# Max-unpooling on one core: the images dealt out in two contiguous parts of 384 and 640, five loads and three stores in place of three and four

## The chip, the core and the metric

The kernel runs on one core of a Trainium2 chip. The metric is device time in microseconds (us) of one execution; nine runs of the kernel before are at hand, and one more execution that was profiled.

## What is computed

The reference undoes a 2x2 max-pooling. Each input value goes to one of four places of a 2x2 block of the output, chosen by its index; the other three places are zero.

```python
output = np.zeros((batch, channels, 2 * h, 2 * w), dtype=np.float32)
for b, c, i, j in ...:
    idx = indices[b, c, i, j]
    output[b, c, 2 * i + idx // 2, 2 * j + idx % 2] = x[b, c, i, j]
```

There are 16 x 64 = 1024 images of 32 x 32 = 1024 values. Per image `x` is 4 KB of float32, the indices are 8 KB, since they lie in HBM as 64-bit integers, and the output is 16 KB. Together 12.58 MB are read and 16.78 MB written.

## The kernel before

**Layout.** Each of the 128 partitions holds `T = 8` consecutive images (L-numbers here are those of the profile). So `x` is one stretch of 32 KB per partition, the indices one of 64 KB, the output one of 128 KB. The whole input fits into the on-chip memory: `x_t` and `idx_t` hold it, and three tiles `out_t` hold two images of output each; the fourth group of two uses the first tile again.

**Loads.** Three DMAs, all on SyncE's queue (SP), are put ahead of SP's preamble by `program.first`: the indices of the first three images of every partition (L110, 24 KB per partition, semaphore `idx_in[0]`), all of `x` (L114, 32 KB per partition, `x_in`), and the indices of the other five images (L116, 40 KB per partition, `idx_in[1]`). In HBM, the rows of L110 and L116 begin 64 KB apart.

**Work.** VectorE waits for `x_in` (L121) and for `idx_in[0]` (L126). Then it walks over the images. For each of the four places of the 2x2 block one `scalar_tensor_tensor` (L137) compares the index with the place's number and multiplies the outcome with `x`, so that the value or a zero lands in a strided part of the output tile. One instruction takes two images (128x2048 elements), but at image 2 and at image 3 it takes one (128x1024), since the second load of indices begins with image 3 and its wait (again L126) stands there. That makes 12 instructions of two images and 8 of one. Ahead of the fourth group VectorE waits until the first store has landed (L132, `stored_0`), since the group writes into the first store's tile. The last instruction of each group raises `made`.

**Stores.** SP waits for `made` to reach 1, 2, 3 and 4, and after each wait issues one store (L150) of two images per partition: 32 KB per partition, rows 128 KB apart in HBM, 4.19 MB in all. At last it lowers `made` (L153), and the wait for the last three stores (L155) is moved to the program's end by `program.last`.

So one queue, SP's, carries all seven transfers in the order of their issue: three loads, four stores. Two things order the work: the loads' landing, for which VectorE waits, and `made`, for which SP waits.

Of the kernel before, what the change touches and what calls it, by code (L numbers as in the profile page):

```python
# [1 line left out]

# [4 lines left out]

P = 128
F32 = mybir.dt.float32
I32 = mybir.dt.int32  # L10


class Program:

    def __init__(self, nc):
        self.nc = nc
        self.block = nc.main_func.blocks[0]  # L20
        self.kernel_block = nc.cur_bb.bb.name

    def __enter__(self):
        ins = self.block.instructions
        self.branches = [i for i in ins if "Branch" in type(i).__name__]
        n = len(ins) - len(self.branches)
        assert all("Branch" in type(ins[k]).__name__ for k in range(n, len(ins)))
        del ins[n:]
        self.nc.switch_bb(self.block.name, parent=None)
        self.symbolic = self.nc._always_lower_symbolic_ap  # L30
        self.nc._always_lower_symbolic_ap = False
        return self

    def first(self, made):
        ins = self.block.instructions
        assert ins[len(ins) - 1].name == made.ins.name
        moved = ins.pop()
        at = next(
            k
            for k, i in enumerate(ins)  # L40
            if i.engine == moved.engine and isinstance(i, mybir.InstDrain)
        )
        ins.insert(at, moved)

    def last(self, made):


        def move(nc):
            ins = self.block.instructions
            at = next(k for k, i in enumerate(ins) if i.name == made.ins.name)  # L50
            nc.main_func.blocks[-1].instructions.append(ins.pop(at))

        self.nc.at_finalize(move)

    def __exit__(self, kind, *_):
        self.nc._always_lower_symbolic_ap = self.symbolic
        if kind is None:
            for b in self.branches:
                self.block.instructions.append(b)
            self.nc.switch_bb(self.kernel_block, parent=None)  # L60


@with_exitstack
def kernel(
    ctx: ExitStack,
    tc: tile.TileContext,
    x: bass.AP,
    indices: bass.AP,
    kernel_size: bass.AP,
    out: bass.AP,  # L70
):
    nc = tc.nc
    assert kernel_size == 2

    B, C, H, W = x.shape
    n_img = B * C
    T = n_img // P
    assert T * P == n_img and C % T == 0

    G = 2  # L80
    NG = T // G
    FIRST = 3
    N = H * W
    x_v = x.rearrange("b (ch t) h w -> (b ch) (t h w)", t=T)
    idx_v = indices.rearrange("b (ch t) h w -> (b ch) (t h w)", t=T).bitcast(I32)
    out_v = out.rearrange("b (ch g t) oh ow -> g (b ch) (t oh ow)", g=NG, t=G)

    x_t = nc.alloc_sbuf_tensor("x_t", [P, T * N], F32).ap()
    idx_t = nc.alloc_sbuf_tensor("idx_t", [P, T * 2 * N], I32).ap()
    out_t = [  # L90
        nc.alloc_sbuf_tensor(f"out_t{g}", [P, G * 4 * N], F32).ap()
        for g in range(NG - 1)
    ]
    out_t.append(out_t[0])

    x_in = nc.alloc_semaphore("x_in")
    idx_in = [nc.alloc_semaphore(f"idx_in{g}") for g in range(2)]
    made = nc.alloc_semaphore("made")
    stored_0 = nc.alloc_semaphore("stored_0")
    stored = nc.alloc_semaphore("stored")  # L100

    x_c = x_t.rearrange("p (t i j) -> p t i j", t=T, j=W)
    idx_c = idx_t.rearrange("p (t i j two) -> p t i j two", t=T, j=W, two=2)[
        :, :, :, :, 0
    ]
    cut = FIRST * 2 * N

    with Program(nc) as program:
        program.first(
            nc.sync.dma_start(out=idx_t[:, :cut], in_=idx_v[:, :cut]).then_inc(  # L110
                idx_in[0], 16
            )
        )
        program.first(nc.sync.dma_start(out=x_t, in_=x_v).then_inc(x_in, 16))  # L114
        program.first(
            nc.sync.dma_start(out=idx_t[:, cut:], in_=idx_v[:, cut:]).then_inc(  # L116
                idx_in[1], 16
            )
        )

        nc.vector.wait_ge(x_in, 16).then_inc(x_in, -16)  # L121
        for t in range(T):
            g, k = t // G, t % G
            if t in (0, FIRST):
                half = int(t == FIRST)
                nc.vector.wait_ge(idx_in[half], 16).then_inc(idx_in[half], -16)  # L126

            if k == 1 and t != FIRST:
                continue
            n = 1 if k == 1 or t + 1 == FIRST else 2  # L130
            if g == NG - 1:
                nc.vector.wait_ge(stored_0, 16).then_inc(stored_0, -16)  # L132
            o_c = out_t[g].rearrange(
                "p (m i two j wo) -> p m i two j wo", m=G, two=2, wo=2, j=W
            )
            for pidx in range(4):
                op = nc.vector.scalar_tensor_tensor(  # L137
                    out=o_c[:, k : k + n, :, pidx // 2, :, pidx % 2],
                    in0=idx_c[:, t : t + n],
                    scalar=pidx,  # L140
                    in1=x_c[:, t : t + n],
                    op0=mybir.AluOpType.is_equal,
                    op1=mybir.AluOpType.mult,
                )
            if k + n == G:
                op.then_inc(made, 1)

        for g in range(NG):
            nc.sync.wait_ge(made, g + 1)
            nc.sync.dma_start(out=out_v[g], in_=out_t[g]).then_inc(  # L150
                stored if g else stored_0, 16
            )
        nc.sync.sem_inc(made, -NG)  # L153
        program.last(
            nc.sync.wait_ge(stored, 16 * (NG - 1)).then_inc(stored, -16 * (NG - 1))  # L155
        )


# [1 line left out]
_INS = ['x', 'indices', 'kernel_size']  # L160
_OUTS = [((16, 64, 64, 64), 'float32')]

_NUMBERS = {'kernel_size': 2}


# [26 lines left out]
```

## Time and profile before

| what | value |
|---|---|
| median of 9 runs | 71.49 us (71.41 to 71.64) |
| the profiled execution: its own time | 71.5 us |
| its span, first to last instruction | 70.2 us |
| VectorE busy, 20 instructions | 35.6 us |
| loads issued at | 0.00, 0.43, 0.90 us |
| from issue to landing of the loads | 9.5, 18.8, 30.5 us |
| stores issued at | 28.4, 37.5, 46.3, 55.1 us |
| from issue to landing of the stores | 12.8, 13.3, 14.2, 15.1 us |

All times in the profile count from the start of the span, which is the issue of the first load. 1.3 us of the execution's own time lie outside of the span. A DMA's landing is the moment at which its completion has raised its semaphore: its issue plus the time to landing.

### The profile page before, as it was taken

To read this page: it belongs to the slowest core of one execution; us is meant where nothing else is said; L and a number is where in the kernel's file an instruction comes from. 1 tells how busy PE (TensorE), PEld (TensorE's weight loads), DVE (VectorE), ACT (ScalarE), POOL (GpSimd) and SP (SyncE) were. 2 spreads that over 40 slices of the span, in tenths; PEclk is the share of its full clock that TensorE was granted. 3 is DMA by queue.
4 is the path that set the end of the run, shared out by engine and by line. 5 is a ranking of instruction groups with operands and counts; after the bars stand their busy time and mean duration, and the time that the engine had idled before them with its cause. 6 is when DMAs were issued, how large, how long until landed. Compare 5 with 4: busy or idle time off the path is not lost.

```text
span 70.2 us, 72 instructions
## 1 busy us (share of the span) xinstructions
DVE 35.6 (51%) x20; POOL 0.2 (0%) x4
## 2 busy tenths in 40 slices
DVE  0000000000099999999999999999999300000000
POOL 1000000000000000000000000000000000000000
DMA  8699996969988999869799797969799897969790
GB/s 224 294 420 434 439 579 299 598 299 523 448 374 374 420 607 467 374 299 560 336 411 486 336 560 318 579 299 579 318 486 411 355 542 336 560 299 579 318 560 37
DMA packets 1008, 29.36 MB, mean 418 GB/s; under 512 B 112, under 2 KB 112, under 8 KB 112
## 3 DMA queue, kind: packets, MB, share of 16 engines
q1 hardware_dynamic: 1008, 29.36, 97.7%
HBM read 12.58 MB, written 16.78 MB: 418 GB/s over the span
## 4 chain that ended last, share of the span: by engine, by line
DVE 46%; DVEq 4%; issue 1%
DVE out_t L137 46%; DVEq L187 4%
## 5 line engine op out<-in xcount | busy, mean ns | idle before, releaser
L137 DVE SCALAR_TENSOR_TENSOR out_t<-idx_t,x_t 128x2048 f32<-128x2048 int32 (+1 forms) x20 | 35.6, 1856 | 19.5 <-DVEq L126 19.5
L173 POOL MEMSET const-uint8-127<- 128x1 uint8 x1 | 0.1, 103 | 0.0
L173 POOL MEMSET const-bfloat16-1.0<- 128x1 bf16 x1 | 0.1, 102 | 0.0
L173 POOL MEMSET const-float32-0.0<- 128x1 f32 x1 | 0.1, 99 | 0.2 <-issue 0.2
L173 POOL MEMSET const-float32-1.0<- 128x1 f32 x1 | 0.1, 99 | 0.0
## 6 DMA issues: line engine op xcount, KB each, us to landing
out_dram<-out_t SPq DMA_DIRECT2D x4, 4096.0 KB, 13.8
idx_t<-in_indices_dram SPq DMA_DIRECT2D x1, 5120.0 KB, 30.5
x_t<-in_x_dram SPq DMA_DIRECT2D x1, 4096.0 KB, 18.8
idx_t<-in_indices_dram SPq DMA_DIRECT2D x1, 3072.0 KB, 9.5
```

What stands on the lines that cost most here:

```text
L137: op = nc.vector.scalar_tensor_tensor(out=o_c[:, k : k + n, :, pidx // 2, :, pidx % 2], in0=idx_c[:, t : t + n], scalar=pidx, in1=x_c[:, t ...
L173: nc = _bacc.Bacc("TRN2", target_bir_lowering=False, num_devices=1)
L187: with _tile.TileContext(nc) as tc:
```

## The change

The images are dealt out to partitions in two parts. Part A is images 0 to 383, three consecutive images per partition; part Z is images 384 to 1023, five per partition. Each part is one unbroken piece of HBM for `x`, for the indices and for the output.

The loads become five, all ahead of SP's preamble as before: indices of A (24 KB per partition) and `x` of A (12 KB), both on semaphore `in_a`; `x` of Z (20 KB) and the indices of the first four images of Z (32 KB), both on `in_z`; the indices of the last image of Z (8 KB, `in_last`).

VectorE's work becomes four steps of four instructions: three images of A after `in_a`; two images of Z after `in_z`; two more, after a wait for its own `made` to reach 2; the last image after `in_last`. That is 4 instructions of 128x3072, 8 of 128x2048 and 4 of 128x1024.

The stores become three: all of A (48 KB per partition, 6.29 MB), the first two images of Z (32 KB, 4.19 MB), and the last three of Z (48 KB, 6.29 MB). Ahead of the first, SP waits for `in_z` besides `made`. The output of the last three lies over input that is used up by then (the whole of A's and the indices of the first two images of Z), in place of an output tile that waits for a store to land; so VectorE's wait for the first store is gone.

```diff
-        nc.vector.wait_ge(x_in, 16).then_inc(x_in, -16)
-        for t in range(T):
-            g, k = t // G, t % G
-            if t in (0, FIRST):
-                half = int(t == FIRST)
-                nc.vector.wait_ge(idx_in[half], 16).then_inc(idx_in[half], -16)
...
-            n = 1 if k == 1 or t + 1 == FIRST else 2
-            if g == NG - 1:
-                nc.vector.wait_ge(stored_0, 16).then_inc(stored_0, -16)
...
+    work = (
+        (x_a, idx_a, 0, A, 0, 0),
+        (x_z, idx_z, 0, Z1, 1, 0),
+        (x_z, idx_z, Z1, Z2 - 1, 2, 0),
+        (x_z, idx_z, Z - 1, 1, 2, Z2 - 1),
+    )
...
+        for tile_, hbm, sem in (
+            (idx_a, idx_v[0], in_a),
+            (x_a, x_v[0], in_a),
+            (x_z, x_v[1], in_z),
+            (idx_z[:, :last_idx], idx_v[1][:, :last_idx], in_z),
+            (idx_z[:, last_idx:], idx_v[1][:, last_idx:], in_last),
+        ):
+            program.first(nc.sync.dma_start(out=tile_, in_=hbm).then_inc(sem, 16))
+
+        for k, (x_s, idx_s, lo, n, o, at) in enumerate(work):
+            if k == 0:
+                nc.vector.wait_ge(in_a, 32).then_inc(in_a, -32)
+            elif k == 1:
+                nc.vector.wait_ge(in_z, 32)
+            elif k == 2:
+                nc.vector.wait_ge(made, 2)
+            else:
+                nc.vector.wait_ge(in_last, 16).then_inc(in_last, -16)
...
-            if k + n == G:
+            if k != 2:
                 op.then_inc(made, 1)
...
+        for k, dst in enumerate(stores):
+            nc.sync.wait_ge(made, k + 1)
+            if k == 0:
+                nc.sync.wait_ge(in_z, 32)
+            nc.sync.dma_start(out=dst, in_=out_t[k]).then_inc(stored, 16)
+        nc.sync.sem_inc(made, -3)
+        nc.sync.sem_inc(in_z, -32)
+        program.last(nc.sync.wait_ge(stored, 48).then_inc(stored, -48))
```

## The prediction

> **What bounds the kernel now.** I first read the head of the page, the transfers' queue and the slices.
>
> ```profile
> span 70.2 us, 72 instructions
> DVE 35.6 (51%) x20; POOL 0.2 (0%) x4
> DMA  8699996969988999869799797969799897969790
> q1 hardware_dynamic: 1008, 29.36, 97.7%
> ```
>
> VectorE (DVE) works half of the span; the one DMA queue keeps the 16 DMA engines busy for 97.7% of it. The slices' sixes are no holes, since a packet here is a whole row of 24 to 40 KB, counted whole in a slice; longer stretches show it:
>
> ```profile
> 0.00:2.00 2.00, 0.00 (x0) 0.20 (x4) 1.00 0.73 197
> 10.00:20.00 10.00, 0.54 (x1) 0.00 (x0) 1.00 1.00 433
> 20.00:30.00 10.00, 10.00 (x6) 0.00 (x0) 1.00 1.05 455
> 30.00:40.00 10.00, 10.00 (x9) 0.00 (x0) 1.00 0.97 419
> 40.00:50.00 10.00, 10.00 (x5) 0.00 (x0) 1.00 0.99 426
> 50.00:60.00 10.00, 5.05 (x3) 0.00 (x0) 1.00 1.07 462
> 68.00:70.20 2.20, 0.00 (x0) 0.00 (x0) 1.00 0.56 238
> ```
>
> The last two columns are DMA share and GB/s. The share stays near 1.00 and the rate near 440 from loads (10 to 30) through to stores (30 to 60); only start and end are slack. Then the chain and the waits:
>
> ```profile
> by line: DVE out_t L137 46.3%; DVEq L187 3.8%; issue 0.8%
> ```
>
> ```profile
> SPq L150 <- DVE out_t L137: 52.3, 4, 26.7
> SPq L155 <- SPq L155: 14.0, 1, 14.0
> ```
>
> The chain names VectorE, but it only follows instructions. The last store is issued at 55.1 us and lands 15.1 us later, though it has 4.19 MB like the first load of x: it stands behind the third store in the queue. So VectorE is not what ends last. The landings are the real clock: 9.5 for the first indices (3.15 MB), 0.43 + 18.8 = 19.2 for x, 0.9 + 30.5 = 31.4 for the other indices, then 28.4 + 12.8 = 41.2, 37.5 + 13.3 = 50.8, 46.3 + 14.2 = 60.5, 55.1 + 15.1 = 70.2. Between them lie 9.7, 12.2, 9.8, 9.6, 9.7, 9.7 us for 4.19, 5.24 and four times 4.19 MB. From 9.5 to 70.2, 26.21 MB move in 60.7 us: **432 GB/s** without a break. That is the price of a byte below.
>
> [...] The rows here are 64 and 128 KB apart[...], and the trace shows no loss from it: x, unbroken, took 9.7 us for 4.19 MB, the stores with rows 128 KB apart took the same. [...]
>
> **The change, part by part.**
>
> *Bytes and rate.* Same 29.36 MB. Contiguous parts: nothing by the rate, as said.
>
> *More rows.* Eight transfers of 128 rows in place of seven: 8 more rows and one more completion on each DMA engine. [...] I take **+0.05**.
>
> *Start.* The first load is again 24 KB per partition. It lands at 9.5 where its bytes need 3.15/432 = 7.3; 2.2 us are issue, first rows and receipt. In finer slices of the DMA engines the first packets show at 0.9 to 1.5 us, the receipt is about 0.4 (the last packets begin by 68.6, a 32 KB row takes 1.2 at the price above, landing 70.2), so some 0.4 us is a slower first row. That its rows lay 64 KB apart could be the reason; the later rows of the same load and of L116 run at full rate, so I take 0, bound **-0.4 to 0**. The fourth and fifth load issue 0.47 us apart like the first three, done by 2.3 us; they push SP's preamble back by 0.9, hidden since nobody needs SP or VectorE before 13 us.
>
> *VectorE's first step.* x of A (1.57 MB) lands 3.6 us after the indices, at 13.1, where VectorE had to wait until 19.2. It starts some 0.25 later as now (landing 19.2, start 19.46). An instruction follows the next after 2.20 us for 2048 elements (35.6 busy for 12 of 2283 and 8 of 1216 ns: each overlaps the next by 0.08) and 1.14 for 1024; for 3072, 2.20 + 1.07 = 3.27. Four end at 13.4 + 4 x 3.27 + 0.08 = **26.6**.
>
> *First store.* It also waits for `in_z`: 2.62 + 4.19 MB after 13.1, 15.8 us, **28.9**. This wait ends last, by 2.3 us; the store is issued at 29.0 rather than 28.4. Queued behind it on SP are the other two stores only. The fifth load (1.05 MB, 2.4 us) is still under way and lands at 31.3. Less 0.4 of receipt, its bytes are through at 30.9 on the slowest DMA engine and some 0.55 earlier, 30.4, on the fastest (the last packets start between 68.0 and 68.6). A transfer's first packets show 0.9 to 1.0 us after its issue: the store's are there at 30.0, which is **0.4 us** ahead of the fastest engine and 0.9 ahead of the slowest. So there is no hole, by a small margin; in the kernel before it was 1.0 and 1.5. The first store now takes 0.1 longer from landing to landing (9.8) than the rest: some friction at the turn from loads to stores, which can stay or go, **-0.15 to +0.15**; I take 0.
>
> *The rest of VectorE.* Step two starts with `in_z` at 29.15 and ends at 29.15 + 4 x 2.20 + 0.08 = 38.0; store two is issued then. A's store (6.29 MB, 14.6 us) occupies the queue until 45.9 in landing time, so this has over 6 us in hand. Step three waits for VectorE's own `made`: behind that wait stand eight instructions and the last store. The wait's latency isn't in the trace; between 0 and the 0.25 seen at 19.2, I take 0.25. Then 8.8 + 4 x 1.14 + 0.08 = 13.4: **51.7**. Store two lands at 45.9 + 9.7 = 55.6, so the last store must be issued by about 55.6 - 0.4 - 0.55 - 1.0 = 53.7. Covered by **2.0 us** (now 3.4: the last is issued at 55.1 and due by 58.5). The four instructions fewer and the removed wait for the first store save nothing: that wait ended at 41.2, ahead of the work it guarded.
>
> *Sum.* 31.3 + (6.29 + 4.19 + 6.29)/432 = 31.3 + 38.8 = 70.1 by rounded landings, which is the span of now. So 70.2 + 0.05 + 0 = 70.25, and the 1.3 us outside of the span stay: the profiled execution's 71.5 becomes 71.55. The median before is 71.49, against 71.5 for the profiled one: **71.53**.
>
> **The rivals.** *No change* (chance 0.52): as summed, 71.35 to 71.63. A measurement can tell 0.2% here, 0.14 us.
>
> *Slower by a hole at the turn* (0.28): the first store is issued only after the landing of `in_z`, and its cover is 2.4 us of the fifth load. It decides if issue to first bytes takes over 1.9 us on the slowest engine, in place of the 1.0 seen at the start. For it: a first row costs 0.4 more than later ones[...]; that is 1.4. Against: even then the slowest engine has half a us left. If everything took twice as long, 2.0 + 0.4, the hole is about 0.5: 72.0. The full restart seen at the start, 2.2 us from issue to landing beyond the bytes, can't come in whole, since 2.4 us of load cover it.
>
> *Faster* (0.20): the first row's 0.4 goes with contiguous rows, or the turn's 0.15, or both: 71.53 - 0.55 = 71.0 at best, 71.2 for the middle. For it: the first load is the one place with a lower rate. Against: a start from empty is slow for any layout.
>
> *VectorE late for the last store* (in the slower 0.28, some 0.03 of it): it would have to lose over 2 us between 13 and 52, say by slower instructions of 3072; the rows scale too evenly for that.
>
> *The change doesn't do what it says*: the wait for `in_z` can't be passed early, as the store of A is ready at 26.6.
>
> **How the numbers follow.** Likeliest is no change, 71.53, own range 71.35 to 71.63. The range of 8 in 10 takes in the middle of the faster case and the slower one's price: 71.1 to 72.0. Faster by over 0.2%: 0.20; within: 0.52; slower: 0.28.
>
> **What would show it.** Right: loads landing at 9.5, 13.1, about 19, 28.9 and 31.3; stores issued at 29.0, 38.0, 51.7; landings 14.6, 9.7 and 14.6 us apart, the last at 70.2; DMA share near 1.00 throughout. A first landing under 9.3 would show that the layout mattered at the start. A stretch of the slices at 30 to 31 us with idle engines, and a first store landing later than 46.1, would show the hole; a last store issued after 53.7, VectorE as the bound. The prediction is wrong if the gap between landings differs from the bytes at 432 GB/s anywhere but at these places.

## The result and the profile after

The changed kernel takes 72.21 us (median of ten runs, 71.88 to 72.37); the kernel before, on the same chips, 71.50. The ratio is 1.0092, 95% interval 1.0077 to 1.0108: **slower by 0.9%**, 0.7 us. The forecast was no change, 71.53, and the range ended at 72.0.

The head of the page after, its DMA slices and its queue:

```profile
span 70.7 us, 69 instructions
DVE 35.5 (50%) x16; POOL 0.2 (0%) x4
DMA  9699999999989899899999998689999999999990
q1 hardware_dynamic: 1152, 29.36, 97.4%
```

The picture is the one of before: the queue is busy nearly all of the span, VectorE half of it. The span has grown from 70.2 to 70.7 us, and nothing on these lines says where. (The profiled execution took 72.02 us; the other nine runs had spans from 70.6 to 71.0, so what was lost differs from one execution to the next.)

The DMA issues of the page after say it, read with the issues in its timeline (loads at 0.00, 0.42, 0.89, 1.36 and about 1.9 us, stores at 29.63, 38.50 and 51.97). The last column is microseconds from issue to landing:

```profile
out_dram<-out_a SPq DMA_DIRECT2D x1, 6144.0 KB, 16.9
out_dram<-inputs SPq DMA_DIRECT2D x1, 6144.0 KB, 18.7
inputs<-in_indices_dram SPq DMA_DIRECT2D x1, 4096.0 KB, 28.2
out_dram<-out_z SPq DMA_DIRECT2D x1, 4096.0 KB, 17.7
inputs<-in_indices_dram SPq DMA_DIRECT2D x1, 3072.0 KB, 10.0
inputs<-in_x_dram SPq DMA_DIRECT2D x1, 2560.0 KB, 18.9
inputs<-in_x_dram SPq DMA_DIRECT2D x1, 1536.0 KB, 13.3
inputs<-in_indices_dram SPq DMA_DIRECT2D x1, 1024.0 KB, 30.1
```

The first load (3072 KB) lands at 10.0 us. Before, the first load, of the same size and with the same 24 KB per row, landed at 9.5:

```profile
idx_t<-in_indices_dram SPq DMA_DIRECT2D x1, 3072.0 KB, 9.5
```

In the changed kernel the landings after the first are 13.7, 19.8, 29.6, about 32.0, 46.5, 56.2 and 70.7: steps of 3.7, 6.1, 9.8, 2.4, 14.5, 9.7 and 14.5 us, each within 0.15 of what its bytes need at 432 GB/s. So the half microsecond was lost before the first landing, and the queue carried it to the end.

Where in the first load, the busy time by stretches of 1 us shows; the last two columns are DMA share and GB/s. Before:

```profile
1.00:2.00 1.00, 0.00 (x0) 0.00 (x0) 1.00 1.46 393
2.00:3.00 1.00, 0.00 (x0) 0.00 (x0) 1.00 0.91 393
3.00:4.00 1.00, 0.00 (x0) 0.00 (x0) 1.00 0.91 393
```

After:

```profile
1.00:2.00 1.00, 0.00 (x0) 0.00 (x0) 1.00 1.68 393
2.00:3.00 1.00, 0.00 (x0) 0.00 (x0) 1.00 0.58 246
3.00:4.00 1.00, 0.00 (x0) 0.00 (x0) 1.00 0.91 393
```

A row is counted where it begins. In both kernels 16 rows begin between 1 and 2 us, as many as the profile counts DMA engines (16 x 24 KB in 1 us are 393 GB/s). Between 2 and 3 us, 16 further rows begin before, and only 10 after (246 GB/s). The first rows took longer, which also shows in the share of 1.68 against 1.46.

The trace's records of single packets give the sizes. The 16 first rows end at 2.64 us on average before and at 2.91 after, the last of them at 2.81 and at 3.31. After that a row takes 0.91 us in both kernels. The landing follows the last of the first rows: it comes 6.7 us after that row has ended, both times. So the half microsecond is the lateness of the slowest first row; on average the first rows ended only 0.27 us later.

The waits after show that nothing else ends late. The first two lines are VectorE's, the third SP's:

```profile
DVE out_a L155 <- DVEq L140: 13.9, 1, 13.9
DVE out_z L155 <- DMA inputs<-in_indices_dram: 2.5, 1, 2.5
SPq L174 <- SPq L174: 17.7, 1, 17.7
```

VectorE starts at 13.9 rather than 19.5, stops for 2.5 us until `in_z` has landed, and SP waits 17.7 us after the issue of the last store, so VectorE is far ahead of the end.

### The profile page after: what moved, and what is told of

The parts are those of the page before. It is cut to its first block, busy times and chain, and to the rows that moved or that the text cites. A ratio compares the mean times of both kernels' runs of the same rounds, so it can differ in the third digit from the quotient of the medians.

```text
span 70.7 us, 69 instructions
## 1 busy us (share of the span) xinstructions
DVE 35.5 (50%) x16; POOL 0.2 (0%) x4
## 2 busy tenths in 40 slices
DMA packets 1152, 29.36 MB, mean 415 GB/s; under 512 B 128, under 2 KB 128, under 8 KB 128
## 3 DMA queue, kind: packets, MB, share of 16 engines
q1 hardware_dynamic: 1152, 29.36, 97.4%
## 4 chain that ended last, share of the span: by engine, by line
DMA 40%; DVE 25%; DVEq 6%; SPq 2%; issue 1%
DMA inputs<-in_indices_dram 40%; DVE inputs L155 13%; DVE out_z L155 13%; DVEq L205 6%; SPq L136 2%
## 5 line engine op out<-in xcount | busy, mean ns | idle before, releaser
L155 DVE SCALAR_TENSOR_TENSOR out_a<-inputs 128x3072 f32<-128x3072 int32 x4 | 13.2, 3354 | 13.9 <-DVEq L140 13.9
L155 DVE SCALAR_TENSOR_TENSOR inputs<-inputs 128x2048 f32<-128x2048 int32 (+1 forms) x8 | 13.4, 1751 | 0.0
L155 DVE SCALAR_TENSOR_TENSOR out_z<-inputs 128x2048 f32<-128x2048 int32 x4 | 8.9, 2285 | 2.5 <-DMA inputs<-in_indices_dram 2.5
## 6 DMA issues: line engine op xcount, KB each, us to landing
out_dram<-out_z SPq DMA_DIRECT2D x1, 4096.0 KB, 17.7
inputs<-in_x_dram SPq DMA_DIRECT2D x1, 1536.0 KB, 13.3
```

Source lines behind the costliest of these rows:

```text
L155: op = nc.vector.scalar_tensor_tensor(out=o_c[:, :, pidx // 2, :, pidx % 2], in0=idx_c, scalar=pidx, in1=x_c, op0=mybir.AluOpType.is_equal ...
```

## The experiments

Times are medians; each ratio is against the kernel before on the same chip, with its 95% interval. In some kernels one load reads its indices from other places of the same tensor. Their outputs are other numbers, but the bytes and the instructions are the same.

**Layout or queue?** Two things at the start differ: the rows of the first load lie 24 KB apart in HBM instead of 64, and four loads instead of two are issued behind it. Theory L blames the first, theory Q the second. First, the kernel before with the unbroken source:

```diff
+    flat = indices.rearrange("b ch h w -> (b ch) (h w)")[: FIRST * P]
+    idx_first = flat.rearrange("(p t) n -> p (t n)", t=FIRST).bitcast(I32)
-            nc.sync.dma_start(out=idx_t[:, :cut], in_=idx_v[:, :cut]).then_inc(
+            nc.sync.dma_start(out=idx_t[:, :cut], in_=idx_first).then_inc(
```

> The kernel before, with one edit: the first load takes its 24 KB rows from one unbroken 3.15 MB of HBM (as the changed kernel does) in place of rows 64 KB apart; it thereby reads the indices of other images, so the first three images of each partition come from wrong indices. Theory L (the layout of the first load in HBM makes the start slow): the start is late as in the changed kernel, first load landing near 10.0 instead of 9.5 us, about 72.0. Theory Q (five loads queued behind each other at the start make it slow): nothing changes, 71.5, first landing 9.5.

Measured: 72.0 us, ratio 1.0088 [1.0058, 1.0118]. One edit of an address pattern makes the kernel before as slow as the changed one. Its line of the DMA issues and its stretch from 2 to 3 us:

```profile
idx_t<-in_indices_dram SPq DMA_DIRECT2D x1, 3072.0 KB, 10.1
```

```profile
2.00:3.00 1.00, 0.00 (x0) 0.00 (x0) 1.00 0.68 295
```

Then the reverse, the changed kernel with only its first load read from rows 64 KB apart:

```diff
+    rows = indices.rearrange("b (ch t) h w -> (b ch) (t h w)", t=A + Z).bitcast(I32)
+    idx_first = rows[:, : A * 2 * N]
-            (idx_a, idx_v[0], in_a),
+            (idx_a, idx_first, in_a),
```

> The changed kernel, with one edit: the first load takes its 24 KB rows from HBM rows 64 KB apart, as the kernel before does; so part A is made from other images' indices. Theory L: the start is repaired, first landing 9.5, about 71.6. Theory Q: the start stays late, first landing near 10.0, about 72.2.

Measured: 71.62 us, ratio 1.0020 [1.0013, 1.0028]. Most of the loss is gone, and the same two lines are nearly those of before:

```profile
inputs<-in_indices_dram SPq DMA_DIRECT2D x1, 3072.0 KB, 9.6
```

```profile
2.00:3.00 1.00, 0.00 (x0) 0.00 (x0) 1.00 0.93 393
```

0.14 us (0.09 to 0.20) are left over the kernel before. Their cause is not shown.

The kernel before with five loads in its own layout:

```diff
+        x_cut, last = FIRST * N, (T - 1) * 2 * N
+        for tile_, hbm, sem in (
+            (idx_t[:, :cut], idx_v[:, :cut], idx_in[0]),
+            (x_t[:, :x_cut], x_v[:, :x_cut], x_in),
+            (x_t[:, x_cut:], x_v[:, x_cut:], x_in),
+            (idx_t[:, cut:last], idx_v[:, cut:last], idx_in[1]),
+            (idx_t[:, last:], idx_v[:, last:], idx_in[1]),
+        ):
+            program.first(nc.sync.dma_start(out=tile_, in_=hbm).then_inc(sem, 16))
```

> The kernel before, its layout kept, with its three loads cut into five of the same sizes and order as in the changed kernel (24, 12, 20, 32 and 8 KB per partition). Theory L: 71.5 plus at most 0.1 for more rows, first landing 9.5. Theory Q: first landing near 10.0, about 72.1.

Measured: 71.60 us, ratio 1.0010 [0.9998, 1.0022], first landing 9.5. Theory Q has fallen; two more transfers cost 0.07 us, if anything.

**The changed kernel with the old dealing**, all else as changed:

```diff
     def sections(ap):
-        flat = ap.rearrange("b ch h w -> (b ch) (h w)")
-        return [
-            part.rearrange("(p t) n -> p (t n)", t=t)
-            for part, t in ((flat[: A * P], A), (flat[A * P :], Z))
-        ]
+        rows = ap.rearrange("b (ch t) h w -> (b ch) (t h w)", t=A + Z)
+        cut = A * ap.shape[2] * ap.shape[3]
+        return [rows[:, :cut], rows[:, cut:]]
```

> The changed kernel with the dealing of the kernel before: A is the first three images of each partition's eight, Z the other five, so rows of loads and stores lie 64 and 128 KB apart in HBM; five loads, three stores, VectorE's four steps and all waits stay. If the layout of the first load is the whole loss: 71.5 to 71.65, first landing near 9.5 us. If later contiguous transfers or the fewer, larger stores had their own share in the loss or a gain: outside of this.

Measured: 71.58 us, ratio 1.0004 [0.9993, 1.0016], first landing 9.6. Five loads, three stores, VectorE's four steps and the new waits together cost nothing that can be measured, and gain nothing. This run turns back the dealing of every transfer; that the first load alone decides rests on the two runs with one edit above.

**What about the distance?** The kernel before, with its first load taking the same 24 KB rows from HBM rows 8 to 56 KB apart, the source pattern changed as in the first experiment (at 8 and 16 KB the rows overlap). Written as one pattern:

```diff
+    src = idx_v[0:1, 0:1]
+    idx_first = bass.AP(tensor=src.tensor, offset=src.offset, ap=[[1 * 2 * N, P], [1, cut]])
-            nc.sync.dma_start(out=idx_t[:, :cut], in_=idx_v[:, :cut]).then_inc(
+            nc.sync.dma_start(out=idx_t[:, :cut], in_=idx_first).then_inc(
```

Here `1 * 2 * N` is 8 KB; 16 KB has a 2 there, and 32 to 56 KB have slices of wider rows to the same effect. Five theories ran against each other: A and D from the start, M and W formed after the run with 40 KB, F after the one with 56 KB:

> The kernel before; the first load takes its 24 KB rows from HBM rows 32 KB apart (wrong indices for the first three images of a partition). Theory D (the denser the rows of the first load lie in HBM, the slower the start): between the two layouts, 71.6 to 71.95, first landing 9.6 to 10.0. Theory A (it is the row distance of 24 KB, not a power of two, against one that is): as before, 71.5, first landing 9.5.

> The kernel before; the first load takes its 24 KB rows from HBM rows 40 KB apart (wrong indices for the first three images of a partition). Theory D: nearer to 71.5 than with 32 KB. Theory A: slow like the unbroken one, 72.0, first landing near 10.0.

> The kernel before; the first load takes its 24 KB rows from HBM rows 48 KB apart (wrong indices for the first three images of a partition). Theory M (a distance with a larger power of two in it starts faster; 24 and 40 KB were slow, 32 and 64 fast, and 48 is a multiple of 16): 71.6 to 71.8, like 32 KB. Theory W (only a pure power of two is fast): 72.1.

> The kernel before; the first load takes its 24 KB rows from HBM rows 56 KB apart (wrong indices for the first three images of a partition). Theories M and W: slow like 24 and 40 KB, 72.0 to 72.2. Theory D (density), weakened by the run with 40 KB: nearly as with 64 KB, 71.5.

> The kernel before; the first load takes 24 KB rows that begin 8 KB apart in HBM, so neighbouring rows overlap (wrong indices for the first three images of a partition). Theory F (mirror: row distances p and 64 - p KB start alike; so far 24 like 40, and now 8 like 56): fast, 71.6, first landing 9.6. Theory D (density: all rows within 1 MB): at least as slow as the unbroken one, 72.0 or more, first landing 10.1 or later.

> The kernel before; the first load takes 24 KB rows that begin 16 KB apart in HBM, so neighbouring rows overlap (wrong indices for the first three images of a partition). Theory F (16 like 48): 72.0, first landing 10.1. Theory D: 72.0 or more, between the run with 8 KB and the unbroken one. By itself this run tells little; beside the one with 8 KB it shows whether the time rises or falls with the distance.

Measured, with two moments from the profiled execution of each: the end of the last of the 16 first rows, by the packet records, and the first landing:

| rows apart, KB | time, us | ratio to 64 KB | last first row ends, us | first landing, us |
|---|---|---|---|---|
| 8 | 71.67 | 1.0039 [1.0024, 1.0054] | 3.05 | 9.8 |
| 16 | 72.14 | 1.0091 [1.0072, 1.0109] | 3.58 | 10.3 |
| 24 (unbroken) | 72.0 | 1.0088 [1.0058, 1.0118] | 3.40 | 10.1 |
| 32 | 71.72 | 1.0030 [1.0018, 1.0042] | 3.27 | 9.9 |
| 40 | 72.19 | 1.0094 [1.0080, 1.0108] | 3.37 | 10.1 |
| 48 | 72.03 | 1.0070 [1.0047, 1.0092] | 3.41 | 10.1 |
| 56 | 71.57 | 1.0008 [0.9995, 1.0020] | 2.88 | 9.6 |
| 64 (before) | 71.5 | 1 | 2.81 | 9.5 |

At every distance the landing comes 6.6 to 6.8 us after the last first row has ended, and the median of the later rows is 0.91 us. What the distance changes is how late the last of the first rows is through.

Theories A, M and W, which look for powers of two, miss: 32 KB was to be as fast as 64 under A, and 56 KB to be slow under M and W. Theory D (density) fits 56 KB but missed at 40 KB, where it had a time nearer to 71.5 than at 32 KB. It falls with 8 KB, where all rows lie within 1 MB and the loss is less than half of that at 16 KB. What fits best is the mirror that theory F named before the runs with 8 and 16 KB: 24 and 40 alike, 16 and 48 alike, 56 free and 8 nearly so. It holds roughly, not to the interval (8 KB is 0.3% above 56 KB), and its two tests are the runs whose rows overlap, which could have an effect of its own.

The start at 8 KB is also of another kind than that at 56 KB. First 8, then 56 KB:

```profile
1.00:2.00 1.00, 0.00 (x0) 0.00 (x0) 1.00 0.74 246
2.00:3.00 1.00, 0.00 (x0) 0.00 (x0) 1.00 1.14 492
```

```profile
1.00:2.00 1.00, 0.00 (x0) 0.00 (x0) 1.00 1.32 369
2.00:3.00 1.00, 0.00 (x0) 0.00 (x0) 1.00 0.94 393
```

Only 10 rows begin between 1 and 2 us at 8 KB, and 15 at 56 KB. By the packet records, the first rows at 8 KB begin at 1.82 us on average and take 1.08 us; at 56 KB they begin at 1.21 and take 1.43. So the two times come about in different ways, and the mirror is no shown mechanism.

**Is it a matter of the indices?** The kernel before with the loads of x and of the first indices exchanged:

```diff
+        program.first(nc.sync.dma_start(out=x_t, in_=x_v).then_inc(x_in, 16))
         program.first(
             nc.sync.dma_start(out=idx_t[:, :cut], in_=idx_v[:, :cut]).then_inc(
                 idx_in[0], 16
             )
         )
-        program.first(nc.sync.dma_start(out=x_t, in_=x_v).then_inc(x_in, 16))
```

> The kernel before, with the load of x (rows of 32 KB, unbroken, so 32 KB apart) issued ahead of the first indices; VectorE waits for both anyway. If the distance of the rows with which the queue starts decides, whatever tensor it is: as with rows 32 KB apart, 71.7. If unbroken rows of any size are slow at the start: 72.0. If it is a matter of the indices alone: 71.5.

Measured: 71.72 us, ratio 1.0028 [1.0016, 1.0040], just as with index rows 32 KB apart (1.0030). Of the three forecasts only that of the distance fits: it goes by the distance of the rows with which the queue starts, not by the tensor. In the kernel before the same x, second in the queue, lost nothing (9.7 us for its 4.19 MB).

**The rows in another order.** Two kernels dealt the rows of the first load to the partitions in another order: partition 8b + a takes row 16a + b. The aim was that the DMA engines read rows side by side in HBM; that this order does so was the author's assumption, since the packet records don't say which engine took which row.

```diff
+    flat = indices.rearrange("b ch h w -> (b ch) (h w)")[: FIRST * P].bitcast(I32)
+    idx_first = flat.rearrange("(lo hi t) n -> hi lo (t n)", t=FIRST, hi=16)
-            nc.sync.dma_start(out=idx_t[:, :cut], in_=idx_v[:, :cut]).then_inc(
+            nc.sync.dma_start(out=idx_t[:, :cut], in_=idx_first).then_inc(
```

The second kernel is the same with `t=T` and `[:, :, :cut]`, rows 64 KB apart.

> The kernel before; the first load takes the same unbroken 3.15 MB of HBM as the changed kernel, but dealt out differently: neighbouring partitions take rows 16 apart[...] (wrong indices for the first three images of a partition). Theory D (what counts is that all lies in 3.15 MB): slow, 72.0. Theory E (what counts is how far apart the rows are that the engines read at the same moment): another time than 72.0[...].

> The kernel before; the first load takes rows 64 KB apart as in the kernel before, but dealt out so that neighbouring partitions take rows 16 apart[...], as in the interleaved run that took 79.1 (wrong indices for the first three images of a partition). If that run's half rate came from the small distance of 24 KB: near 71.5 to 72. If it came from the dealing itself[...]: the first load at half rate again, near 79.

Measured: 79.09 us, ratio 1.106 [1.1045, 1.1074], and 79.5 us, ratio 1.1112 [1.1089, 1.1135]. The rate during the first load, and once it is over, in the first of them:

```profile
5.00:15.00 10.00, 0.00 (x0) 0.00 (x0) 1.00 1.02 214
20.00:30.00 10.00, 2.80 (x2) 0.00 (x0) 1.00 1.07 459
```

Half the rate at full DMA share, for the whole load and not for a first row, and with 64 KB (229 GB/s in the same stretch) as with 24. So these two runs miss their aim: they say nothing on the distance in HBM. It is this form of transfer that halves the rate, by the order of its rows or by its access pattern, which has one dimension more; the two runs don't part these. Why it does is not shown.

**Putting off the later loads.** The changed kernel, with SP issuing the third to fifth load after the first has landed:

```diff
-            (idx_a, idx_v[0], in_a),
+            (idx_a, idx_v[0], in_i),
...
-            program.first(nc.sync.dma_start(out=tile_, in_=hbm).then_inc(sem, 16))
+            load = nc.sync.dma_start(out=tile_, in_=hbm).then_inc(sem, 16)
+            if sem in (in_i, in_a):
+                program.first(load)
+            if sem is in_a:
+                nc.sync.wait_ge(in_i, 16)
```

> The changed kernel, with SP issuing the third to fifth load only after the first has landed (the second is queued by then, so the DMA engines do not run dry). Theory L: the start stays late, first landing near 10.0, about 72.2. Theory Q: repaired or better, first landing 9.5 or less, about 71.6.

Measured: 73.22 us, ratio 1.0249 [1.0227, 1.0272]. Both theories missed: the first landing stayed at 10.0, as L said, but 1.0 us more was lost. The DMA engines didn't run dry: by the rows that begin there their share was 1.03 from 10 to 12 us and 1.01 from 12 to 14. The third load was issued at 10.1 and lands 10.8 later, at 20.9, where the changed kernel has 19.8:

```profile
inputs<-in_x_dram SPq DMA_DIRECT2D x1, 2560.0 KB, 10.8
inputs<-in_x_dram SPq DMA_DIRECT2D x1, 1536.0 KB, 13.3
```

The second load landed at 0.43 + 13.3 = 13.7, so the third was in the queue 3.6 us ahead of that. Two more runs asked whether the distance of its rows did this; the deferral is the same edit, on the kernel with the old dealing and on the one with only its first load 64 KB apart.

> The changed kernel with the dealing of the kernel before (71.58) and with SP issuing the third to fifth load only after the first has landed. In the changed kernel that deferral cost 1.0 us, all of it lost by the landing of the third load (x of Z, unbroken 20 KB rows). Theory R (a load that is issued late meets the same trouble of row distances as the first one): here the third load's rows lie 32 KB apart, so little is lost, 71.6 to 71.9. Rival (late issue costs by itself): 72.5, as much over 71.58 as the deferral cost there.

> The changed kernel with the first load's rows 64 KB apart (71.62; part A is made from other images' indices) and the same deferral; the third load keeps its unbroken 20 KB rows. Theory R: 72.4 to 72.7. Rival (late issue costs by itself): 72.5 as well; this run tells only beside the other, and shows that the third load's loss doesn't hang on a bad first load.

Measured: 72.22 us, ratio 1.0111 [1.0090, 1.0132], 0.64 us above its kernel without the deferral; and 71.99 us, ratio 1.0072 [1.0056, 1.0088], 0.37 above its own. Theory R falls: it had 71.6 to 71.9 for the first and 72.4 to 72.7 for the second, and the rows 32 KB apart lost more than the unbroken rows in the run beside it, though less than the 1.0 of the unbroken rows in the changed kernel. The rival's 72.5 was missed too, by 0.3 and 0.5. What the three runs show is that the late issue costs 0.4 to 1.0 us, though at that moment the second load had still over 3 us to go.

The packet records place this loss. Without the deferral each of the 128 rows of the third load took 0.76 us, in all three kernels. With it 35, 23 and 24 of them took longer, the first ones above all, up to 1.78 us. From the second landing to the third it is 7.2, 6.7 and 6.4 us with the deferral, and 6.1 in the changed kernel. So the third load, issued late, met slow first rows though the queue was not empty. It was issued 2.5, 2.9 and 3.0 us ahead of its first row, and lost 1.0, 0.6 and 0.4 us; that a longer lead makes the loss smaller is a guess from three runs, and why there is a loss stays open.

**The first store later.** The kernel before, with the two images of the first group made one at a time:

```diff
-            if k == 1 and t != FIRST:
+            if k == 1 and t not in (1, FIRST):
                 continue
-            n = 1 if k == 1 or t + 1 == FIRST else 2
+            n = 1 if t <= FIRST else 2
```

> The kernel before, with VectorE making the first group's two images one at a time: four instructions more, which puts off the first store by 8 x 1.14 - 4 x 2.20 = 0.3 us, to 28.7. Theory of the turn (a store that reaches the DMA engines early, in the midst of the loads' last rows, costs 0.1 us there): 71.4 to 71.5. Rival (the turn costs what it costs): 71.5. It has no bearing on the start, first landing 9.5.

Measured: 71.52 us, ratio 1.0001 [0.9990, 1.0012]; the first store was issued at 28.8. VectorE's four more instructions didn't lengthen the time. The two forecasts overlap, and the interval is 0.1 us to either side, so the run does not decide whether the turn can be made cheaper.

No run was faster than the kernel before, and none pointed to a kernel that would be.

## Why the prediction was wrong, step by step

- **The bound** was right: one queue at the rate of 432 GB/s sets the end, and the steps between landings after the first are within 0.15 us of what their bytes need.
- **Contiguous parts, "nothing by the rate"**: right for the stream, whose landings keep to 432 GB/s as before, and a wrong question for the start.
- **Start: the step that failed.** "That its rows lay 64 KB apart could be the reason; the later rows of the same load and of L116 run at full rate, so I take 0, bound -0.4 to 0." The term was +0.5 us in the profiled execution (first landing 10.0 instead of 9.5) and about +0.7 in the medians. That the first row is slow was read rightly: 0.4 us was worked out, and by the packet records it takes 1.46 us against 0.91. "A start from empty is slow for any layout" held for the eight distances tried: the first rows took 1.08 to 1.85 us on average, the later ones 0.91 in the median. But the layouts differ, and the slowest first row counts. Two errors are in the term. The bound excluded a loss without a reason: the trace showed that the first rows were slow in one layout, which says that the layout may matter there, not that 64 KB is the worst. And the full rate of later rows was taken as evidence for first rows; the runs show that the same pattern costs at the start what it doesn't cost in the stream (x first, 71.72; x second, 71.5).
- **The suspect** was the wide distance of before, never the narrow one of after. In the runs 64 KB, with 71.5 us, was the best of the eight distances, with 56 KB (71.57) within the interval; 24 KB had 72.0.
- **More rows, +0.05**: consistent, but an estimate of the author's; what a row costs is not shown. One more transfer of 128 rows brought 144 packets, 1152 in place of 1008. Two more loads cost 0.07 us (-0.01 to 0.16), all of the new structure 0.03 (-0.05 to 0.11).
- **VectorE's first step**: four instructions of 3072 took 13.16 us, as worked out; they ended at 27.0 instead of 26.6, since the start was late.
- **No hole at the turn**: right. The store issued at 29.63 lands 14.5 us after the fifth load, 14.6 forecast. So the rival that had the slower case, with 72.0 as its price, had the wrong mechanism though nearly the right time.
- **The wait for its own `made`** costs VectorE hardly anything: step two ends at 29.57 + 8.90 = 38.47 and step three starts at 38.50. The value of 0.25 was too high; it was off the path either way. The last store was issued at 51.97, against 51.7, with 0.5 of late start in it.
- **The sum** had 70.25; with +0.5 in place of 0 at the start it is 70.75, and the span is 70.7.

**Shown**: the loss comes from the row distance of the first load in HBM, in both directions, and it is lost in the first rows, the last of which ends at 3.31 in place of 2.81 us. The rest of the structure costs 0.03 us (-0.05 to 0.11). **Not shown**: what in the memory or in the engines makes one distance better than another, and what a distance over 64 KB does; whether any layout streams faster than 432 GB/s; where the 0.14 us come from that are left when only the first load is turned back; and why the loss differs between executions (0.4 to 0.9 us in the ten runs; the profiled one, with 0.5, was the second fastest).

## What to carry to other kernels

Where one queue of transfers keeps the same rate from its first landing to its last, as here with 432 GB/s, look at what happens before the first landing: here the half microsecond that the first transfer lost (10.0 us in place of 9.5) stood whole in the span (70.7 in place of 70.2), and the contiguous pattern was not the quickest (72.0 us against 71.5). Where a trace shows a slow place in one layout only, bound another layout's cost there on both sides. To tell layout from structure, change the source pattern of one transfer and leave all else; the output then has other numbers.

## What the runs showed of the hardware

- The start of the first load from empty depended on how far apart its rows lay: 24 KB rows 64 or 56 KB apart landed at 9.5 and 9.6 us, rows 8 or 32 KB apart at 9.8 and 9.9, rows 16, 24, 40 or 48 KB apart at 10.1 to 10.3. Once under way, all distances ran at the same rate, 0.91 us for a row in the median.
- The 16 first rows didn't end alike: in the changed kernel they ended between 2.59 and 3.31 us, and the landing came 6.7 us after the last of them.
- The third to fifth load, issued at about 10 us while the second had over 3 us to go, cost 0.4 to 1.0 us against the same loads issued at the start; early rows of the third took up to 1.78 us in place of 0.76.
- A load with the partitions dealt as 16 x 8 on the HBM side ran at 214 GB/s (rows 24 KB apart) and 229 GB/s (64 KB), about half of the 432 of the plain loads.
